# A decoder trunk on one core: another start of the first norm, and the output stored in eight pieces

## The chip, the core and the metric

The kernel runs on one core of one Trainium2 chip. The core has a matrix engine (PE, with its weight loads shown apart as PEld), a vector engine (DVE), a scalar engine (ACT), a general engine (POOL), a sequencer that here only issues transfers (SP), and 16 DMA engines between the chip's memory (HBM) and the core's own memory (SBUF). ACT can issue transfers too, on a queue of its own. PE writes to PSUM, eight banks of 128 x 512 numbers.

The metric is device time in microseconds (us). Of the kernel before there are three timed runs and one profiled execution.

## The reference

Two layers over 256 tokens of width 2048. Each of the four sub-layers (two mixers, two feed-forward blocks) starts with a norm whose scale and shift come from a conditioning row `c`, and ends in a gated residual add. What matters here is the first norm, the row `c`, and the end:

```python
def rms_norm(x, eps=EPS):
    xf = x.astype(jnp.float32)
    return (xf * lax.rsqrt(jnp.mean(xf * xf, -1, keepdims=True) + eps)).astype(x.dtype)

def ada_modulation(c, w, b):
    mod = (jax.nn.silu(c) @ w + b)[:, None, :]
    shift, scale, gate = jnp.split(mod, 3, axis=-1)
    return shift, scale, gate

def reference(x, c, ada_mix_w, ada_mix_b, ...):
    for i in range(DEPTH):
        shift, scale, gate = ada_modulation(c, ada_mix_w[i], ada_mix_b[i])
        h = rms_norm(x) * (1.0 + scale) + shift
        ...                                   # a mixer: h @ w_in, recurrences, @ w_out
        x = x + gate * y
        shift, scale, gate = ada_modulation(c, ada_ffn_w[i], ada_ffn_b[i])
        h = rms_norm(x) * (1.0 + scale) + shift
        x = x + gate * swiglu(h, ffn_w1[i], ffn_w3[i], ffn_w2[i])
    return rms_norm(x) * final_norm_w
```

## The kernel before

The activations lie transposed: 16 tiles (`kt`) of 128 channels x 256 tokens. A product takes a 128 x 128 tile of weights as the stationary operand and 256 tokens as the moving one. For precision each weight tile is split into a high and a low part, `whi` (ACT, a rounding copy) and `wlo` (DVE, a subtraction), and so are the activations (`hhi`, `hlo`); a product is three matmuls: `whi` with `hhi`, `whi` with `hlo`, `wlo` with `hhi`.

**The modulation.** `silc` holds silu(c), the same row of 2048 numbers on all 128 partitions. One modulation value per channel is a multiply-and-sum of a weight row with `silc` on DVE. For the first norm these are 32 tiles of 128 x 2048 (`ini`, 1 MB each, six buffers): for each `kt` one for the scale (a small addition of 1 follows) and one for the shift. The remaining modulations come later, in halves of 1024 columns (`adat`).

**The first stage.** The input `x` arrives in one transfer. ACT squares it tile by tile, PE sums the squares over the channels (the squares are the stationary operand, a block of ones from the constants `cst` the moving one), DVE and POOL raise the sums to the power -1/2 (`rpow`, lines 806 to 809), PE spreads the result over the partitions (`bcast_tok`), ACT copies it to `rb`. From there on, `kt` by `kt`: POOL multiplies `x` by `rb` (`normed`), ACT applies scale and shift and rounds to `hhi`, POOL subtracts to get `hlo` (`first`), and `lin_slab` multiplies with the first 14 weight tiles of that `kt`, which come in two transfers of 7 (448 KB each, four buffers `raw`).

**What sets the order.** Every engine works through its instructions in the order of the program; a wrapper adds that dependence to each call, and so all instructions carry its line, 374, in the profile. The order itself is planned while the program is written out: a list `seq` says in which order the big pieces are loaded and processed (for the first stage: the two `ini` tiles of kt 0, those of kt 1, the two weight pieces of kt 0, the two `ini` tiles of kt 2, the weight pieces of kt 1, and so on). `split_next` processes the next item of that list: for an `ini` tile the multiply-and-sum on DVE, for a weight piece the copy `whi` on ACT; `low_parts` then emits the `wlo` that are due on DVE. `issue_raw` issues the next transfers on SP, strictly in the list's order, when a buffer is free. A cost model (`Clock`, one time per engine) decides between steps that could both come next; its price for a full-precision matmul with 128 stationary columns is

```python
            return max(430.0 if nn < 60 else 214.0, 1.68 * nn)
```

in nanoseconds, where `nn` is the number of moving columns. `split_next(4)` in line 1957 processes the first four `ini` tiles before the squares; the lines from 1961 on are the norm.

**The end.** `rstd_x` makes the last norm's factor in the same manner into a PSUM bank, DVE multiplies `x` by it in four pieces of 128 x 1024, and SP stores each piece.

Of the kernel before, what the change touches and what calls it, by code (L numbers as in the profile page):

```python
# [10 lines left out]
F32 = mybir.dt.float32  # L11
F32R = mybir.dt.float32r
AF = mybir.ActivationFunctionType
ALU = mybir.AluOpType
# [4 lines left out]
P = 128  # L19
T = 256  # L20
KT = 16
# [62 lines left out]
SLAB0, SLAB1, SLABF = len(FIRST0), 7, {0: 14, 1: 8}  # L84
# [50 lines left out]
def halves(n):  # L135

    return [n] if n <= 8 else [(n + 1) // 2, n // 2]
# [260 lines left out]
def trunk(ctx: ExitStack, tc: tile.TileContext, I, out):  # L398
    nc = tc.nc
    clock = Clock()  # L400
    V, S, G, PE, SP = (Ordered(tc, e, clock) for e in (nc.vector, nc.scalar, nc.gpsimd, nc.tensor, nc.sync))
    pool = lambda name, bufs=1, **k: ctx.enter_context(tc.tile_pool(name=name, bufs=bufs, **k))
    cp = pool("cp")
# [10 lines left out]
    def nm(s):  # L414
        uid[0] += 1
        return f"{s}_{uid[0]}"

    def mm(out_, lhsT, rhs, start, stop):
        PE.matmul(out_, lhsT, rhs, start=start, stop=stop)
# [10 lines left out]
    banks = [pp_.tile([P, 512], F32, name=f"bank{q}") for q in range(8)]  # L430
# [5 lines left out]
    def bank(keep=False, spare=SPARE):  # L436

        if keep and len(mine) == 1:
            force(lambda: len(busy) < 8 - spare)
        q = min((q for q in range(8) if q not in busy),  # L440
                key=lambda q: clock.since(bname[q]))
        busy.add(q)
        if not keep:
            mine[-1].append(q)
        return banks[q]
# [48 lines left out]
    def force(stop):  # L494

        while not stop():
            c = min((c for c in chains if not blocked(c)), key=lambda c: c.ready)
            fill_ada(c.ready - IDLE)
            step(c)
# [8 lines left out]
    prm = cp.tile([P, NPRM], F32, name="prm")  # L508
    rows = cp.tile([P, NROW], F32, name="rows")
    silc = cp.tile([P, 2048], F32, name="silc")  # L510
    SP.dma_start(silc, I["crow"].to_broadcast([P, 2048]))
    S.dma_start(x0, I["xT"])
    S.dma_start(cst, I["cst"])
    S.dma_start(prm, I["prm"])
    S.activation(silc, silc, AF.Silu)
    hhi = cp.tile([P, KT, T], F32R, name="hhi")
    hlo = cp.tile([P, KT, T], F32R, name="hlo")
    h2 = (hhi, hlo)
# [1 line left out]
    def K(name, n=None):  # L520
        w = dict(_CST)[name] if n is None else n
        return cst[:, CST[name]:CST[name] + w]
# [4 lines left out]
    ones1 = K("ones", 64)  # L527
    gmask = cst[:, CST["tri"]:CST["tri"] + 384]

    def prc(name, j=0, n=1):  # L530
        return prm[:, COL[name] + j:COL[name] + j + n]
# [4 lines left out]

    half_neg = cp.tile([P, 4], F32, name="half_neg")
    G.memset(half_neg, -0.5)
    half_pos = cp.tile([P, 4], F32, name="half_pos")
    G.memset(half_pos, 0.5)  # L540
    mod = cp.tile([P, 4, 48], F32, name="mod")


# [51 lines left out]
    def issue_raw(upto=-1):  # L595

        while st["raw"] < len(seq):
            it = seq[st["raw"]]
            free, names = (rfree, rname) if it[0] == "w" else (ifree, iname)
            if not free:  # L600
                return
            q = min(free, key=lambda q: clock.since(names[q]))
            if st["raw"] > upto and clock.since(names[q]) > clock.at(ET.PE) + QUEUE:
                return
            free.remove(q)
            if it[0] == "w":
                SP.dma_start(rawt[q][:, :it[2] * P], it[1])
            else:
                l, r, n = it[1:]
                SP.dma_start(init[q], I["ada"][l, 16 * r + n].rearrange("e p f -> p e f"))  # L610
            raws[st["raw"]] = q
            st["raw"] += 1

    def free_raw(q):
        rfree.append(q)
        issue_raw()
# [48 lines left out]
    def split_next(rows=None):  # L665

        while st["item"] < len(seq):
            if rows is not None:
                rows -= 1
                if rows < 0:  # L670
                    return
            i = st["item"]
            issue_raw(i)
            force(lambda: st["raw"] > i)
            it, q = seq[i], raws[i]
            if it[0] == "a":
                raws.pop(i)
                st["item"] += 1
                l, r, n = it[1:]
                t = init[q].rearrange("p e f -> p (e f)")  # L680
                o = mod[:, l, 16 * r + n:16 * r + n + 1]
                V.tensor_tensor_reduce(t, t, silc, 1.0, prc("adab", 48 * l + 16 * r + n), ALU.mult, ALU.add, o)
                if r == 1:
                    V.tensor_scalar(o, o, 1.0, None, ALU.add)
                known.add((l, r, n))
                ifree.append(q)
                issue_raw()
                hook(it[1:4])
                if not after_ada:
                    hook()  # L690
                continue
            n = min(PIECE, it[2] - st["off"])
            if 0 < it[2] - st["off"] - n < PIECE // 2:
                n = (it[2] - st["off"] + 1) // 2
            a, b = st["off"] * P, (st["off"] + n) * P
            hi = wp.tile([P, PIECE * P], F32R, tag="whi", name=nm("whi"), bufs=PARTS)
            lo = wp.tile([P, PIECE * P], F32R, tag="wlo", name=nm("wlo"), bufs=PARTS)
            S.activation(hi[:, :b - a], rawt[q][:, a:b], AF.Copy)
            parts.append((hi, lo, n))
            st["off"] += n  # L700
            end = st["off"] == it[2]
            if end:
                st["off"] = 0
                st["item"] += 1
                raws.pop(i)
            lows.append((hi, lo, a, b, q, end))
            return

    def low_parts():

        while lows:
            hi, lo, a, b, q, end = lows.pop(0)
            V.tensor_tensor(lo[:, :b - a], rawt[q][:, a:b], hi[:, :b - a].bitcast(F32), ALU.subtract)
            if end:
                free_raw(q)
# [3 lines left out]
    def hook(row=None):  # L719

        while hooks and not st["hold"]:
            hooks.pop(0)()
        if row in after_ada:
            hooks.append(after_ada.pop(row))
# [118 lines left out]
    def rstd_x():  # L843
        squares(True)
        ps = bank(True)
        for n in range(2):
            for q in "az":
                mm(ps[:, 64 * n:64 * n + 64], sqa[q][:, n * P:(n + 1) * P], ones1, q == "a", q == "z")
        sqa.clear()
        r = cp.tile([P, 2], F32, tag="rstd", name=nm("rstd"), bufs=2)  # L850
        rpow(r, ps[:, 0:128:64], 2, 1.0 / 2048, EPS)
        release(ps)
        rb = bank(True)
        bcast_tok(rb, r)
        return rb
# [301 lines left out]
    def open_x(name):  # L1157
        xg[name] = tc.tile_pool(name=name, bufs=1, side="right", reuse_waits="tile")
        x = xg[name].__enter__().tile([P, KT, T], F32, name=name)
        xt[name] = x  # L1160
        return x

    def close_x(name):
        xg[name].__exit__(None, None, None)
# [775 lines left out]
    t0 = open_x("tin")  # L1940
# [17 lines left out]
    pq = bank(True)  # L1958
    for kt in range(KT):

        S.activation(t0[:, kt, :], x0[:, kt, :], AF.Square)
    for n in range(2):
        for kt in range(KT):
            mm(pq[:, 64 * n:64 * n + 64], t0[:, kt, n * P:(n + 1) * P], ones1, kt == 0, kt == KT - 1)
    r0 = cp.tile([P, 2], F32, tag="rstd", name=nm("rstd"), bufs=2)
    rpow(r0, pq[:, 0:128:64], 2, 1.0 / 2048, EPS)
    release(pq)
    pq = bank(True)
# [18 lines left out]
    x = layer0(pre_)  # L1987
# [1 line left out]
    layer1(x, "t0b")  # L1989
    ffn(3, x, "t1", None)  # L1990
    rb = rstd_x()
    for q in range(4):
        o = x[:, 4 * q:4 * q + 4, :]
        V.tensor_tensor(o, o, rb[:, 0:T].unsqueeze(1).to_broadcast([P, 4, T]), ALU.mult)
        SP.dma_start(out[:, 4 * q:4 * q + 4, :], o)
    close_x("x0")


# [13 lines left out]
```

## Time and profile before

| | |
|---|---|
| timed runs, median (lowest to highest) | 2975.08 us (2968.41 to 2989.75) |
| profiled execution, its own time | 2977.68 us |
| its span | 2976.0 us |
| PE busy | 2865.2 us, 96% of the span |
| DVE busy | 2176.3 us, 73% |
| ACT busy | 1432.3 us, 48% |
| POOL busy | 218.4 us, 7% |
| DMA | 706.29 MB, mean 237 GB/s |

Busy times are sums over one engine's instructions. PE's instructions overlap, so a busy PE need not be a PE at its best pace. The shares are means over the whole span; the first 140 us, which hold the first norm and the first slab of weights, are read by themselves below. In the views of instructions a row gives start, duration, engine, line, operation, output and inputs, how many instructions were merged, and in brackets the engine's idle time before it with what ended that. In the views of stretches a row gives the busy time of PE, PEld, DVE, ACT and POOL (with the number of instructions), then PE's granted clock, the busy share of the DMA engines and the GB/s they moved.

### The profile page before, as it was taken

The numbers are of one execution on the slowest core, as the hardware profiler recorded it, in microseconds if no ns is written. First come the engines' busy times: TensorE is split into PE (matmuls) and PEld (weight loads), VectorE is DVE, ScalarE is ACT, GpSimd is POOL, SyncE is SP. The second block draws the span as 40 slices with busy tenths as digits, with TensorE's granted clock in tenths as the row PEclk, the third lists the DMA queues.
The fourth block names the chain that finished last, engine by engine and source line by source line (L and its number), as shares of the span: only waits on it lengthen the run. The fifth ranks groups of instructions, "written<-read, shape, count | busy, mean of one in ns | idle before, by whom it ended". The sixth has DMA issues, their size and how long they took to land. (4 is left out here: it accounts for less than half of the span.)

```text
span 2976.0 us, 61340 instructions
## 1 busy us (share of the span) xinstructions
PE 2865.2 (96%) x25114; PEld 2800.0 (94%) x25114; DVE 2176.3 (73%) x3379; ACT 1432.3 (48%) x2363; POOL 218.4 (7%) x250
## 2 busy tenths in 40 slices
PE   6789999998999999999999999999999999999998
PEld 6788898888999999999999999999999999999998
DVE  6987887987878877667688778788867544555454
ACT  3354545544444444444456655554444444444444
POOL 3400001001000000000101001011010000000001
PEclk9999999998999999999999999999999999999999
DMA  9965464587989998788865556676867555555554
GB/s 387 357 203 190 161 207 167 176 279 273 338 278 338 330 310 274 263 272 266 269 228 205 200 200 211 213 250 232 296 224 247 203 180 176 198 189 187 184 177 157
DMA packets 237306, 706.29 MB, mean 237 GB/s; under 512 B 36912, under 2 KB 55648, under 8 KB 236768
## 3 DMA queue, kind: packets, MB, share of 16 engines
q1 hardware_dynamic: 236448, 699.46, 68.3%
q8 instruction: 196, 3.21, 0.4%
q10 hardware_dynamic: 576, 2.92, 0.2%
q14 instruction: 86, 0.70, 0.1%
HBM read 695.70 MB, written 6.58 MB: 236 GB/s over the span
## 5 line engine op out<-in xcount | busy, mean ns | idle before, releaser
L374 DVE TENSOR_TENSOR wlo<-raw,whi 128x1024 fp32r<-128x1024 f32 (+3 forms) x1005 | 1123.8, 1123 | 548.9 <-ACT whi L374 545.8
L374 PE MATMUL bank<-hhi,whi 128*128 128x256 f32 x5568 | 1467.5, 286 | 21.4 <-ACT whi L374 18.1
L374 PE MATMUL bank<-hlo,whi 128*128 128x256 f32 x5568 | 1446.1, 282 | 2.6 <-DVE hlo L374 2.4
L374 ACT ACTIVATE whi<-raw 128x1024 fp32r<-128x1024 f32 (+3 forms) x1005 | 971.6, 972 | 913.0 <-PE bank L374 733.6
L374 PE MATMUL bank<-hhi,wlo 128*128 128x256 f32 x5568 | 1117.4, 283 | 33.3 <-DVE wlo L374 33.0
L374 PEld LDWEIGHTS bank<-hhi,whi 128*128 128x128 f32 x5568 | 1057.3, 190 | 38.4 <-ACT whi L374 21.2
L374 PEld LDWEIGHTS bank<-hlo,whi 128*128 128x128 f32 x5568 | 1057.1, 190 | 6.0 <-DVE hlo L374 3.8
L374 PEld LDWEIGHTS bank<-hhi,wlo 128*128 128x128 f32 x5568 | 855.6, 190 | 42.5 <-DVE wlo L374 39.0
L374 PE MATMUL bank<-ghi,whi 128*128 128x256 f32 x1408 | 351.2, 282 | 0.0
L374 PE MATMUL bank<-glo,whi 128*128 128x256 f32 x1408 | 351.2, 282 | 0.0
L374 PEld LDWEIGHTS bank<-glo,whi 128*128 128x128 f32 x1408 | 265.1, 188 | 0.0
L374 PEld LDWEIGHTS bank<-ghi,whi 128*128 128x128 f32 x1408 | 265.1, 188 | 0.0
L374 PE MATMUL bank<-ghi,wlo 128*128 128x256 f32 x1408 | 229.7, 282 | 0.0
L374 DVE CUSTOM_DVE_ANT_0 adat<-adat,silc,adap 128x1024 f32<-128x1024 f32 x160 | 212.7, 1329 | 21.1 <-DMA adat<-in_ada 20.3
L374 DVE CUSTOM_DVE_ANT_0 adat<-adat,silc,prm 128x1024 f32<-128x1024 f32 x160 | 211.4, 1322 | 14.8 <-DMA adat<-in_ada 14.6
L374 PEld LDWEIGHTS bank<-ghi,wlo 128*128 128x128 f32 x1408 | 193.8, 188 | 0.0
L374 ACT ACTIVATE ghi<-fg 128x256 fp32r<-128x256 f32 x88 | 36.8, 418 | 161.8 <-DVE fg L374 161.8
L374 DVE SCALAR_TENSOR_TENSOR w<-pad,prm,w 128x256 f32<-128x256 f32 x216 | 109.5, 509 | 5.2
L374 DVE CUSTOM_DVE_ANT_0 ini<-ini,silc,prm 128x2048 f32<-128x2048 f32 x32 | 84.7, 2648 | 15.9 <-DMA prm<-in_prm 15.9
L374 DVE SCALAR_TENSOR_TENSOR x<-bank,mod,x 128x256 f32<-128x256 f32 x106 | 50.7, 482 | 49.0 <-PE bank L374 49.0
L374 DVE TENSOR_TENSOR glo<-fg,ghi 128x256 fp32r<-128x256 f32 x88 | 37.4, 425 | 42.6 <-ACT ghi L374 42.6
L374 PE MATMUL bank<-ylo,whi 128*128 128x256 f32 x256 | 67.0, 284 | 0.8 <-DVE ylo L374 0.8
(261 smaller groups left out, 1994.5 us busy)
## 6 DMA issues: line engine op xcount, KB each, us to landing
raw<-in_ffn SPq DMA_DIRECT2D x324, 512.0 KB, 4.2
adat<-in_ada SPq DMA_DIRECT2D x320, 512.0 KB, 5.0
raw<-in_in SPq DMA_DIRECT2D x238, 512.0 KB, 4.1
raw<-in_ffn SPq DMA_DIRECT2D x128, 384.0 KB, 3.8
raw<-in_ffn SPq DMA_DIRECT2D x128, 320.0 KB, 3.3
raw<-in_out SPq DMA_DIRECT2D x75, 512.0 KB, 4.7
ini<-in_ada SPq DMA_DIRECT2D x32, 1024.0 KB, 11.1
raw<-in_in SPq DMA_DIRECT2D x48, 448.0 KB, 4.2
```

Source lines behind the costliest of these rows:

```text
L374: r = f(*a, **k)
```

## The change

- The row `c` is loaded once, to one partition (8 KB), where before it was loaded to all 128 (1 MB). Four matmuls with a stationary row of 0.5 spread it over the partitions, into banks 0 to 3, and four activations of 512 columns with a scale of 2 make `silc` from them. The constant 0.5 is set earlier on POOL for that.
- The parameters `prm` (345.5 KB) are loaded ahead of `x` and of the constants on ACT's queue, where before they were last.
- The sums of squares use 16 columns of ones where before they used 64; the results are read at the same places.
- The two weight pieces of kt 0 are split (`whi` on ACT behind the squares, `wlo` on DVE ahead of `rpow`) where before this was done in `lin_slab`.
- The output is multiplied and stored in eight pieces of 128 x 512, whose transfers are issued by SP and ACT in turn.

```diff
@@ trunk
-    SP.dma_start(silc, I["crow"].to_broadcast([P, 2048]))
+
+    SP.dma_start(silc[0:1, :], I["crow"])
+    S.dma_start(prm, I["prm"])
     S.dma_start(x0, I["xT"])
     S.dma_start(cst, I["cst"])
-    S.dma_start(prm, I["prm"])
-    S.activation(silc, silc, AF.Silu)
+    half_pos = cp.tile([P, 4], F32, name="half_pos")
+    G.memset(half_pos, 0.5)
+    for q in range(4):
+        PE.matmul(banks[q], half_pos[0:1, 0:1].to_broadcast([1, P]), silc[0:1, 512 * q:512 * (q + 1)],
+                  start=True, stop=True)
+    for q in range(4):
+        S.activation(silc[:, 512 * q:512 * (q + 1)], banks[q], AF.Silu, scale=2.0)
...
     half_neg = cp.tile([P, 4], F32, name="half_neg")
     G.memset(half_neg, -0.5)
-    half_pos = cp.tile([P, 4], F32, name="half_pos")
-    G.memset(half_pos, 0.5)
...
         S.activation(t0[:, kt, :], x0[:, kt, :], AF.Square)
+
+    for n in range(len(halves(SLAB0))):
+        split_next()
+    low_parts()
     for n in range(2):
         for kt in range(KT):
-            mm(pq[:, 64 * n:64 * n + 64], t0[:, kt, n * P:(n + 1) * P], ones1, kt == 0, kt == KT - 1)
+            mm(pq[:, 64 * n:64 * n + 16], t0[:, kt, n * P:(n + 1) * P], ones1[:, 0:16], kt == 0, kt == KT - 1)
...
-    for q in range(4):
-        o = x[:, 4 * q:4 * q + 4, :]
-        V.tensor_tensor(o, o, rb[:, 0:T].unsqueeze(1).to_broadcast([P, 4, T]), ALU.mult)
-        SP.dma_start(out[:, 4 * q:4 * q + 4, :], o)
+    for q in range(8):
+        o = x[:, 2 * q:2 * q + 2, :]
+        V.tensor_tensor(o, o, rb[:, 0:T].unsqueeze(1).to_broadcast([P, 2, T]), ALU.mult)
+        (SP, S)[q % 2].dma_start(out[:, 2 * q:2 * q + 2, :], o)
```

## The prediction

> **What bounds the kernel now.** I read the stretches of the first 140 us first, because all parts of the change but one lie there, then the instructions of DVE, ACT and PE in order of time, and the last 10 us at the end.
>
> ```profile
> span 2976.0 us, 61340 instructions
> 10.00:30.00 20.00, 14.81 (x69) 14.62 (x69) 9.81 (x11) 7.02 (x18) 0.70 (x1) 1.00 1.03 413
> 30.00:50.00 20.00, 16.17 (x102) 14.62 (x102) 15.48 (x13) 8.59 (x13) 11.40 (x10) 0.91 0.96 357
> 50.00:130.00 80.00, 60.80 (x457) 58.55 (x455) 79.62 (x78) 31.97 (x44) 40.01 (x20) 0.94 1.03 416
> 132.00:134.00 2.00, 0.64 (x5) 0.64 (x6) 2.00 (x4) 1.02 (x2) 0.48 (x1) 1.00 0.38 154
> ```
>
> From 50 to 130 us DVE is busy 79.62 us of 80 while PE is busy 60.80: DVE sets the pace of the first slab. In the same stretch the DMA engines move 416 GB/s at a busy share of 1.03, so they are full as well. Which of the two would stop first if the other were ahead is the main question. Traffic falls off in the stretch from 132 us: 154 GB/s for 2 us is 0.31 MB, or 0.7 us at 416, so the last `ini` tile has landed at about 132.7.
>
> ```profile
> 15.86 2.35 DVE L374 CUSTOM_DVE_ANT_0 ini<-ini,silc,prm 128x2048 f32<-128x2048 f32 x1 [15.86 <-DMA prm<-in_prm]
> ...
> 23.22 2.35 DVE L374 CUSTOM_DVE_ANT_0 ini<-ini,silc,prm 128x2048 f32<-128x2048 f32 x1
> ...
> 28.04 0.16 DVE L374 TENSOR_SCALAR rpow<-bank 128x2 f32<-128x2 f32 x1 [2.46 <-PE bank L374]
> 34.45 3.03 DVE L374 TENSOR_TENSOR wlo<-raw,whi 128x896 fp32r<-128x896 f32 x2 [6.24 <-ACT whi L374]
> 37.40 2.83 DVE L374 CUSTOM_DVE_ANT_0 ini<-ini,silc,prm 128x2048 f32<-128x2048 f32 x1
> ...
> 42.62 2.09 DVE L374 TENSOR_TENSOR wlo<-raw,whi 128x896 fp32r<-128x896 f32 x2
> 44.62 2.83 DVE L374 CUSTOM_DVE_ANT_0 ini<-ini,silc,prm 128x2048 f32<-128x2048 f32 x1
> ...
> 102.75 2.08 DVE L374 TENSOR_TENSOR wlo<-raw,whi 128x896 fp32r<-128x896 f32 x2
> ...
> 137.17 2.34 DVE L374 CUSTOM_DVE_ANT_0 ini<-ini,silc,prm 128x2048 f32<-128x2048 f32 x1
> ```
>
> These are DVE's instructions, in order of time. It waits 15.86 us for the parameters, works four `ini` tiles until 25.6, waits 2.46 us for the sums of squares (`rpow`), then 6.24 us for the first `whi`, and from 34.45 on hardly waits until the last `ini` tile ends at 137.17 + 2.34 = 139.5. So what the change does to DVE is judged by where the row of 44.62, the first `ini` tile of kt 3, goes: all later work of the slab hangs on it in a closed row, and what comes after the slab is PE's and hangs on the slab.
>
> **The squares and `rpow`.**
>
> ```profile
> 13.53 0.20 ACT L374 ACTIVATE zeros<-cst 128x1 fp32r<-128x1 f32 x1 [0.52 <-DMA cst<-in_cst]
> 13.64 5.00 ACT L374 ACTIVATE tin<-xin 128x256 f32<-128x256 f32 x16
> 30.37 0.38 ACT L374 ACTIVATE rb<-bank 128x256 f32<-128x256 f32 x1 [11.73 <-PE bank L374]
> ...
> 33.48 2.62 ACT L374 ACTIVATE whi<-raw 128x896 fp32r<-128x896 f32 x3
> 14.09 13.92 PE L374 MATMUL bank<-cst,tin 128*128 128x64 f32 x64 [14.09 <-ACT tin L374]
> 158.72 0.61 PE L374 MATMUL bank<-ggg,cst 128*128 128x16 f32 x2 [5.29 <-DVE ggg L374]
> L374 PE MATMUL bank<-ggg,cst x2: 375/385/395, 158.7 to 159.0; 128*128 128x16 f32 x2
> ```
>
> PE needs 13.92 us for 32 sums, two instructions each: 0.2175 us from one instruction to the next. ACT's 16 squares take 5.00 us and are not the limit. Does a block of 16 columns go faster than one of 64? One product of that shape is in the trace, the last two rows: two instructions take 0.61 us together and the second lasts 0.375 to 0.395, so they start 0.215 to 0.235 apart. That is the pace of the 64 columns, and I take it: fewer columns gain nothing, 13.92 us stay. (The bounds: a quarter of it, a gain of 10.4 us on PE, of which ACT's 5.00 us would let through 8.9; and twice as much, the slower rival below.)
>
> When do the squares start? ACT's `zeros`, which waits for `cst`, stands ahead of them in ACT's order, at 13.53. `cst` was second on ACT's queue and becomes last. The queue carries the same three loads, and its last one, `prm`, let DVE go at 15.86; so 15.86 is the late bound for `cst`, 2.3 us later. The 1.05 MB of `silc` no longer compete; had all of them stood ahead, `cst` would come 2.5 us earlier at 413 GB/s, the early bound. I take 14.3, 0.8 later, nearer the late end because the queue's own bytes ahead of `cst` grow. `rpow` then comes at 28.84 instead of 28.04.
>
> **The row `c` and the parameters.**
>
> ```profile
> L374 PE MATMUL bank<-mxw,mbtok 128*128 128x512 f32 x16 | 8.2, 592 | 0.0
> silc<-in_crow SPq DMA_DIRECT2D x1, 1024.0 KB
> 11.26 0.81 SPq L374 DMA_DIRECT2D raw<-in_in  x2
> DMA to landing us min/median/max: 5.1/8.5/11.9
> L374 ACT ACTIVATE mstate<-bank 128x512 f32<-128x512 f32 x8 | 4.8, 595 | 3.3 <-PE bank L374 3.3
> DMA to landing us min/median/max: 3.2/3.3/3.4
> ```
>
> The nearest matmuls to the four new ones are of 512 columns too: 0.51 us an instruction, two a product, so eight take 4.1 us; if PE starts at half that pace, 8.2. ACT takes 0.6 us for 512 columns out of a bank. Small loads (the last row, those of 64 KB through `gscr`) land 3.3 us after issue, and the row is issued first: there at 4 us. So `silc` is ready between 9 and 13 us, and DVE starts then instead of at 15.86, if the first 1 MB of `ini` has landed. That gain of 3 to 7 us is worth nothing by itself: DVE's next fixed point is `rpow`, and it idled 2.46 us ahead of it already. It makes room: the four `ini` tiles are done at the latest at 25.6 as before, more likely at 22, since 1.05 MB fewer at 413 GB/s let all tiles land 2.5 us earlier.
>
> **The first weights split ahead of `rpow`.** The two `whi` go into the 11.73 us in which ACT waits (30.37); two of the three in the row of 33.48 take 1.8 us. The two `wlo` (2.09 us, row of 42.62) go ahead of `rpow` on DVE. `rpow`, and with it POOL, PE and ACT, is now queued behind them. The pieces were issued at 11.26 and 11.65; the latest landing of any piece of the first 60 us took 11.9 us, so they are there at 23.6 at the latest, `whi` ends at 25.4, `wlo` at 26.5, ahead of 28.84. So that wait costs nothing; if the cover were gone, each us of delay would cost one.
>
> What is late next: behind `rpow` DVE now goes straight to the `ini` tiles of kt 2, at 29.0 instead of 37.40. They take 2.35 and 2.83 us with POOL beside them, until 34.3 with their small additions. Then come the `wlo` of kt 1. Their `whi` stand on ACT behind the first two `hhi`, in the place of the row of 33.48, which came 5.44 us after `rpow`: 34.28. The first takes 0.9 us, so `wlo` starts at 35.2, after 0.9 us of waiting, and the pair ends at 37.3. There the first tile of kt 3 starts: 37.3 against 44.62, **7.3 us earlier**. The 6.24 us of waiting go, the two `wlo` of kt 0 move to where DVE idled, and 0.8 us of later `rpow` is paid.
>
> **Can the DMA follow?** The last tile landed at 132.7. It gains 2.5 us from the missing 1.05 MB, and the dip from 30 to 50 us (357 instead of 416 GB/s, 20 us x 59 = 1.18 MB, 2.8 us), which came when DVE stood still and freed no buffer, should close: 127.4. DVE will want it at 137.17 - 7.3 = 129.9. For the weight pieces,
>
> ```profile
> 97.73 2.05 ACT L374 ACTIVATE whi<-raw 128x896 fp32r<-128x896 f32 x2 [1.29 <-DMA raw<-in_in]
> ```
>
> ACT waited for landing and ended at 99.78, with 3.0 us to spare before DVE's `wlo` at 102.75. DVE gets 7.3 ahead, the transfers 5.3, so 2.0 of the 3.0 go. Both margins hold, narrowly. I charge nothing, and take the DMA as the first rival.
>
> **The end.**
>
> ```profile
> 2966.80 1.22 DVE L374 TENSOR_TENSOR x<-x,bank 128x1024 f32<-128x1024 f32 x1 [1.59 <-PE bank L374]
> L374 DVE TENSOR_TENSOR part<-part,bank 128x512 f32<-128x512 f32 x3 | 2.0, 675 | 0.0
> 2968.00:2969.00 1.00, 0.00 (x0) 0.00 (x0) 1.00 (x2) 0.00 (x0) 0.00 (x0) 0.80 0.14 53
> 2973.00:2974.00 1.00, 0.00 (x0) 0.00 (x0) 0.00 (x0) 0.00 (x0) 0.00 (x0) 0.50 1.03 410
> ```
>
> The stores' traffic starts near the end of the first of these two stretches and is still full in the second: the transfer is the limit, not DVE. The first piece is ready after 0.68 us instead of 1.22, so the stores start and end 0.5 us earlier. Bounds: nothing, or a loss of 0.5, if rows of 2 KB move a tenth slower than rows of 4 KB over 5 us; a gain of 1 if the shorter last piece lands sooner. I take 0.5.
>
> **The sum**, against the profiled execution: 2977.68 - 7.3 - 0.5 = 2969.9. That execution lies 2.6 above the median of the runs shown, and so the forecast against that median is 2975.08 - 7.8 = **2967.3**.
>
> **The rivals.**
>
> The DMA is the limit (chance 0.20). With shares of 1.03 from 10 to 30 and from 50 to 130 us it may not catch up the dip; then only the 2.5 us of missing bytes come through, with the dip 5.3. In the middle, with the end: 2975.08 - 3.9 - 0.5 = 2970.7. For it speaks the full share; against it, that the last tile lay landed for 137.17 - 132.7 = 4.5 us.
>
> PE runs the squares at full pace (0.08).
>
> ```profile
> 2964.41 0.39 PE L374 MATMUL bank<-cst,sqacc 128*128 128x64 f32 x2
> 2964.63 0.39 PE L374 MATMUL bank<-cst,sq 128*128 128x64 f32 x2
> ```
>
> At the end of the kernel the same sums take 0.22 us for two instructions, half of the 0.435 at the start. If the four new dense products bring PE to that pace, the squares take 7.0 us and `rpow` waits only for DVE, near 24.5, 4.3 before 28.84; DVE gains up to 7.3 + 4.3 = 11.6, the transfers hold that to about 127.4 + 2.3 = 129.7 for the last tile's end, 9.8 before: 2975.08 - 9.8 - 0.5 = 2964.8. [...]
>
> Narrow products are slow (0.07), the way it gets slower. The kernel's own cost model prices under 60 columns at 430 and 64 at 214: twice. At 0.87 us a sum, the 32 take 27.8 us, `rpow` comes at 42.8, the first `whi` of kt 1 ends at 42.8 + 5.4 + 0.9 = 49.1, `wlo` at 51.3, in place of 44.62: 6.7 later, less 0.5: 2975.08 + 6.2 = 2981.3. It turns from gain to loss where a sum takes 0.435 + 7.3 / 32 = 0.66 us. The row of 158.72 speaks against it.
>
> The planner hands it back (0.15). Its PE clock runs 32 x 216 ns = 6.9 us later after the squares, and banks 0 to 3 are taken earlier; order and banks after the slab may differ. One wait of the length of the row of 158.72 (5.29 us) won or lost: 2975.08 - 7.8 + 5.3 = 2972.6, or 2962.0.
>
> **How the numbers follow.** The forecast (0.50) gives 2967.3. All cases lie between 2962 and 2981.3. The runs shown scatter from 6.7 below to 14.7 above their median, which no case explains; half of each goes to the bounds: low, the planner's better end less some 4 us, 2958; high, the slower rival, 2981.3, which a scatter of 7 above the DMA and planner cases also fills, 2981. A change below 1% (29.8 us), about what a measurement of this kernel can tell from none, holds for every case; outside it only an unforeseen order of the whole program would lead: faster 0.03, same 0.94, slower 0.03.
>
> **What would show it.** Right: DVE's first `ini` tile starts between 9 and 13 us; `whi` and `wlo` of kt 0 lie before `rpow`; `rpow` near 28.8 with 64 matmuls at 0.22 us; the tile of kt 3 near 37.3; the last tile's end near 132; DMA with no dip between 30 and 50. Wrong: DVE waiting for `ini` or for `whi` behind `raw` in the slab (the DMA); a squares row of 7 us or of 28; `rpow` waiting for `wlo`; or the slab earlier and the end not.

## The result and the profile after

The changed kernel takes 2930.10 us (median of 6 runs, 2919.82 to 2947.00). The kernel before, run beside it and counted with the runs shown earlier, takes 2981.69 us (6 runs, 2968.41 to 2989.75). The ratio is 0.9842, with a 95% interval of 0.9816 to 0.9867: 51.6 us less after, where 7.8 were predicted, and the time lies below the predicted range of 2958 to 2981.3 us. The profiled execution after took 2919.82 us, with a span of 2918.0.

The first view is the view of stretches of the kernel after. The columns are those of the prediction: PE, PEld, DVE, ACT and POOL busy with their instructions, granted clock, DMA share, GB/s.

```profile
10.00:30.00 20.00, 13.84 (x64) 13.73 (x64) 13.63 (x14) 7.30 (x20) 1.57 (x1) 1.00 1.02 414
30.00:50.00 20.00, 17.91 (x130) 16.93 (x131) 15.01 (x15) 9.74 (x15) 13.71 (x13) 1.00 1.01 405
50.00:130.00 80.00, 59.88 (x446) 57.70 (x446) 79.62 (x78) 29.50 (x42) 37.62 (x20) 0.91 1.00 404
780.00:880.00 100.00, 100.00 (x885) 100.00 (x884) 81.17 (x110) 50.26 (x70) 0.00 (x0) 1.00 0.87 306
1040.00:1080.00 40.00, 40.00 (x340) 40.00 (x339) 30.59 (x44) 15.99 (x21) 0.00 (x0) 1.00 0.88 301
2300.00:2400.00 100.00, 100.00 (x885) 100.00 (x884) 51.99 (x58) 44.80 (x56) 0.00 (x0) 1.00 0.58 193
```

And the last three of these stretches in the kernel before:

```profile
780.00:880.00 100.00, 100.00 (x855) 100.00 (x854) 77.79 (x106) 48.69 (x68) 0.00 (x0) 1.00 0.86 292
1040.00:1080.00 40.00, 40.00 (x340) 40.00 (x339) 30.16 (x44) 15.88 (x20) 0.00 (x0) 1.00 0.91 300
2300.00:2400.00 100.00, 100.00 (x845) 100.00 (x844) 52.53 (x60) 43.27 (x54) 0.00 (x0) 1.00 0.57 197
```

Between 780 and 880 us, and between 2300 and 2400, PE never stops, before or after, and its granted clock is 1.00. The change touches no instruction there. Yet after it PE starts 885 matmuls in 100 us, one each 113.0 ns, where before it started 855 and 845, one each 117.0 and 118.3 ns. Both stretches belong to products with `hhi` and `hlo`. The stretch from 1040 to 1080 us belongs to products with `ghi` and `glo`, the operands of the feed-forward's second half, and there nothing changed: 340 in 40 us, 117.6 ns.

Is it less waiting? The groups of PE's instructions say no. Before:

```profile
L374 PE MATMUL bank<-hhi,whi 128*128 128x256 f32 x5568 | 1467.5, 286 | 21.4 <-ACT whi L374 18.1
L374 PE MATMUL bank<-ghi,whi 128*128 128x256 f32 x1408 | 351.2, 282 | 0.0
```

After (columns: busy us, mean ns of one | idle time ahead of it, and what ended that):

```profile
L374 PE MATMUL bank<-hhi,whi 128*128 128x256 f32 x5568 | 1437.1, 282 | 22.6 <-ACT whi L374 19.1
L374 PE MATMUL bank<-ghi,whi 128*128 128x256 f32 x1408 | 351.1, 281 | 0.0
```

PE idles as long ahead of the `hhi` products as before, 22.6 us to 21.4. It is the busy time that fell, by 30.4 us in this one of three groups of the kind, and the `ghi` group did not move.

Worked out from the trace, from the first to the last matmul with the named operands (us):

| products with | before | after | less |
|---|---|---|---|
| `hhi`, `hlo` of the first mixer | 34.5 to 986.5 = 952.0 | 35.1 to 971.2 = 936.1 | 15.9 |
| `ghi`, `glo`, first of four parts (the others are alike) | 125.4 | 125.5 | -0.1 |
| `hhi`, `hlo` of the first feed-forward block | 247.9 | 242.0 | 5.9 |
| `hhi`, `hlo` of the second mixer | 623.2 | 608.8 | 14.4 |
| `yhi`, `ylo` | 92.8 | 92.9 | -0.1 |
| `hhi`, `hlo` of the second feed-forward block, two parts | 251.2 + 248.0 | 240.1 + 239.6 | 19.5 |

Some 4 us of the first row are the changed start; nearly all the rest of the gain is spread over the whole kernel wherever `hhi` or `hlo` is an operand.

What sets these two apart from `ghi` and `yhi`? The edit moves a line that reserves memory. `half_pos`, 16 bytes on each partition in a slot of 32, is reserved ahead of `hhi` and `hlo` instead of behind them. So `hhi` begins at byte 31168 of each partition instead of 31136, and `hlo` at 47552 instead of 47520 (addresses of the built programs). `whi`, `wlo`, `ghi`, `glo`, `yhi` and `ylo` lie where they lay, each at a multiple of 128 bytes.

### The profile page after: what moved, and what is told of

The parts are those of the page before. It is cut to its first block, busy times and chain, and to the rows that moved or that the text cites. A ratio compares the mean times of both kernels' runs of the same rounds, so it can differ in the third digit from the quotient of the medians.

```text
span 2918.0 us, 61372 instructions
## 1 busy us (share of the span) xinstructions
PE 2812.5 (96%) x25122; PEld 2741.8 (94%) x25122; DVE 2170.1 (74%) x3383; ACT 1430.5 (49%) x2366; POOL 219.7 (8%) x250
## 5 line engine op out<-in xcount | busy, mean ns | idle before, releaser
L374 PE MATMUL bank<-hhi,whi 128*128 128x256 f32 x5568 | 1437.1, 282 | 22.6 <-ACT whi L374 19.1
L374 PE MATMUL bank<-hlo,whi 128*128 128x256 f32 x5568 | 1415.2, 278 | 4.3 <-DVE hlo L374 3.0
L374 PE MATMUL bank<-hhi,wlo 128*128 128x256 f32 x5568 | 1097.4, 280 | 31.0 <-DVE wlo L374 30.6
L374 PEld LDWEIGHTS bank<-hhi,wlo 128*128 128x128 f32 x5568 | 843.4, 189 | 40.0 <-DVE wlo L374 36.3
```

What stands on the lines that cost most here:

```text
L374: r = f(*a, **k)
```

## The experiments

The theory was that the place of `hhi` and `hlo` sets the pace, and the rival that the changed instructions do, by another order or by work that they trigger later. The first two runs separate these: one has the new place alone, the other all of the new instructions at the old place.

**The new place alone.**

```diff
@@ before
+    half_pos = cp.tile([P, 4], F32, name="half_pos")
     hhi = cp.tile([P, KT, T], F32R, name="hhi")
...
-    half_pos = cp.tile([P, 4], F32, name="half_pos")
     G.memset(half_pos, 0.5)
```

> The kernel before, with one line moved: the tile of the constant 0.5 is reserved ahead of hhi and hlo, so that these two lie 32 bytes further on in SBUF, at 31168 instead of 31136; no instruction, no order and no bank changes. If the place of hhi and hlo makes most of the gain: PE's matmuls with hhi and hlo in the two-projection stretches start 0.113 us apart (443 in 50 us) instead of 0.117 (428), and the time is some 40 to 45 us below before, ratio about 0.986. If the order that the planner made or the choice of banks makes it: no change, ratio 1.000 within 0.002. If it is the new start and end: no change either.

2932.59 us (4 runs), ratio to before 0.9857 (0.9830 to 0.9884): 46.7 us of the gain come from a line that issues nothing. The stretches of this kernel (PE alone: busy, instructions, clock, DMA share, GB/s):

```profile
780.00:880.00 100.00, 100.00 (x882) 1.00 0.88 306
1040.00:1080.00 40.00, 40.00 (x340) 1.00 0.89 303
2300.00:2400.00 100.00, 100.00 (x885) 1.00 0.60 194
```

They are those of the kernel after: 882 and 885, with 340 for `ghi`.

**The new instructions at the old place.**

```diff
@@ after
+    hhi = cp.tile([P, KT, T], F32R, name="hhi")
+    hlo = cp.tile([P, KT, T], F32R, name="hlo")
+    zeros = cp.tile([P, 1], F32R, name="zeros")
+    half_neg = cp.tile([P, 4], F32, name="half_neg")
     half_pos = cp.tile([P, 4], F32, name="half_pos")
...
-    hhi = cp.tile([P, KT, T], F32R, name="hhi")
-    hlo = cp.tile([P, KT, T], F32R, name="hlo")
...
-    zeros = cp.tile([P, 1], F32R, name="zeros")
...
-    half_neg = cp.tile([P, 4], F32, name="half_neg")
```

> The changed kernel with hhi, hlo, zeros and half_neg reserved ahead of the constant 0.5, so that all tiles lie where they lay before; all instructions, their order and their banks are those of the changed kernel. If the place of hhi and hlo makes most of the gain: only the start and the end are left of it, 5 to 9 us, ratio 0.997 to 0.998, and 428 matmuls in 50 us. If planner or banks make it: the whole gain stays, ratio 0.984, 443 in 50 us.

2972.84 us (10 runs), ratio 0.9984 (0.9970 to 0.9999): the whole of what the prediction had costed is worth 6.4 us of 2979.27 by the medians, with an interval from 0.3 to 8.9.

```profile
780.00:880.00 100.00, 100.00 (x836) 1.00 0.84 285
2300.00:2400.00 100.00, 100.00 (x845) 1.00 0.62 203
```

836 and 845: the old pace. The two effects add up, 46.7 + 6.4 = 53.1 us against 51.6 measured for both.

**Which places?** Four more kernels move `hhi` by reserving other small tiles, or the parameter rows, ahead of it or behind it: to 31200, 31232, 30592 and 30656. One diff for all; which lines are moved differs:

```diff
@@ before: 31200 with the first two lines, 31232 with all three
+    half_pos = cp.tile([P, 4], F32, name="half_pos")
+    half_neg = cp.tile([P, 4], F32, name="half_neg")
+    zeros = cp.tile([P, 1], F32R, name="zeros")
     hhi = cp.tile([P, KT, T], F32R, name="hhi")
     hlo = cp.tile([P, KT, T], F32R, name="hlo")
@@ 30592 with the first line, 30656 with all three, and besides
-    rows = cp.tile([P, NROW], F32, name="rows")
...
     hlo = cp.tile([P, KT, T], F32R, name="hlo")
+    rows = cp.tile([P, NROW], F32, name="rows")
```

> The kernel before with the tiles of 0.5 and -0.5 reserved ahead of hhi and hlo: both lie 64 bytes further on, at 31200 and 47584, 32 past a multiple of 64 as before. If a start on a multiple of 64 bytes is what counts: the old pace, 0.117 us a matmul, and the time of before within 0.4%. If only the old place was bad: 0.113 us and some 40 us less.

> The kernel before with the tiles of 0.5, -0.5 and zeros reserved ahead of hhi and hlo: both lie 96 bytes further on, at 31232 and 47616, multiples of 64, 128 and 256. If a start on a multiple of 64 is what counts: 0.113 us a matmul and some 40 us less than before. If it is the place within 128 or 256 bytes (the fast one lies 64 past a multiple of 128, while ghi, at a multiple of 128, goes at 0.118): the old pace, 0.117, and no gain.

> The kernel before with the tile rows reserved behind hhi and hlo and that of 0.5 ahead: hhi and hlo start at 30592 and 46976, multiples of 128, 896 past a multiple of 1024. If the place within 128 bytes decides: slow, 0.117 to 0.120 us a product with hhi or hlo. If any place away from that of the weights over 1024 bytes is fast: 0.113. If a start on a multiple of 64 were enough, it would be fast too, but 31232 has spoken against that.

> The kernel before with rows reserved behind hhi and hlo, and the tiles of 0.5, -0.5 and zeros ahead: hhi and hlo start at 30656 and 47040, 64 past a multiple of 128 and 192 past one of 256, but 960 past one of 1024. If the place within 128 or 256 bytes decides: fast, 0.113 us, some 45 us below before. If the place over 1024 bytes, against the weights, decides: slow, 0.117 to 0.120.

One run each: 2989.28 us at 31200, 3001.84 at 31232, 2990.19 at 30592, 2945.02 at 30656. The row of 780 to 880 us of each, in this order:

```profile
780.00:880.00 100.00, 100.00 (x848) 1.00 0.86 294
```

```profile
780.00:880.00 100.00, 100.00 (x836) 1.00 0.85 283
```

```profile
780.00:880.00 100.00, 100.00 (x845) 1.00 0.87 290
```

```profile
780.00:880.00 100.00, 100.00 (x885) 1.00 0.88 303
2300.00:2400.00 100.00, 100.00 (x851) 1.00 0.56 187
```

Only 30656 has 885, and it is, like 31168, 64 bytes past a multiple of 128. The others are 96, 0 and 0 past one, and 31136 is 32 past. But 30656 did not hold the pace: 851 in the later stretch.

**The same for `ghi`.** If this is right, `ghi` and `glo` are at a bad place in both kernels.

```diff
@@ after; a second kernel reserves [P, 208], 832 bytes
+            fp.tile([P, 16], F32, name=f"gpad{l}")
             ghi = fp.tile([P, NHH, T], F32R, name=f"ghi{l}")
```

> The changed kernel with 64 unused bytes ahead of ghi and glo, so that they start at 120512 and 143040, 64 past a multiple of 128 (192 past one of 256), like hhi and hlo in the changed kernel; nothing else differs. If the place within 128 or 256 bytes decides: the products with ghi and glo go at 0.113 us instead of 0.1187, 4224 of them, 23 us less than the changed kernel, ratio to before about 0.976. If the place against that of the weights (whi, wlo), seen over 1024 bytes, decides, or something that belongs to hhi and hlo alone: no change from the changed kernel, ratio 0.984.

> The changed kernel with 832 unused bytes ahead of ghi and glo: they start at 121280 and 143808, at 448 past a multiple of 1024, where hhi and hlo of the changed kernel stand too, and 64 short of where whi and wlo stand. If the place within 1024 bytes, that is against the weights, decides: products with ghi and glo at 0.113 us instead of 0.1187. If the place within 128 bytes decides: 121280 is 64 past a multiple of 128, so 0.113 as well, and only the run with 64 bytes tells the two apart. If neither: 0.1187.

With 64 bytes 2912.45 us (4 runs), ratio to before 0.9757 (0.9724 to 0.9791), below both kernels; with 832 bytes 2912.29 (one run). The stretch of `ghi`, first with 64 and then with 832 bytes:

```profile
1040.00:1080.00 40.00, 40.00 (x356) 1.00 0.94 324
```

```profile
1040.00:1080.00 40.00, 40.00 (x355) 1.00 0.93 327
```

356 and 355 instead of 340: 112.4 and 112.7 ns a product.

**The place itself, or the distance from the weights?** In all kernels so far `whi` and `wlo` lay at multiples of 128. So "64 past a multiple of 128" and "64 from the weights, modulo 128" could not be told apart. The next kernel moves the weights.

```diff
@@ after
     adat = [wp.tile([P, 1024], F32, name=f"adat{q}") for q in range(ADAS)]
+    wp.tile([P, 16], F32, name="wpad")
```

> The changed kernel with 64 bytes reserved behind the adat tiles. hhi and hlo stay where the changed kernel has them (64 bytes past a multiple of 128); the weight pieces whi and wlo, until now at multiples of 128, and everything behind them (ini, ghi, glo, yhi, ylo) move 64 bytes up. Theory A, what counts is the place of the streamed operand (hhi, ghi) by itself: hhi products stay at 113.3 ns (885 in 100 us) and ghi products go to 113.3 as well (355 in 40 us instead of 339), about 2912 us. Theory B, what counts is the distance of the streamed operand from the weights: hhi products fall back to 118 to 120 ns (836 to 855 in 100 us) and ghi products stay at 118.7, about 2972 us.

2988.42 us (one run), 16 us more than theory B expected; the pace decides between the two.

```profile
780.00:880.00 100.00, 100.00 (x845) 1.00 0.86 289
1040.00:1080.00 40.00, 40.00 (x340) 1.00 0.89 304
2300.00:2400.00 100.00, 100.00 (x845) 1.00 0.63 205
```

`hhi` has not moved, and its products are back at 845; `ghi` has moved to 64 past a multiple of 128, and gains nothing, since the weights have moved with it. The theory of the place itself falls. Its mirror image settles it: the operands at multiples of 128, the weights 64 past one.

```diff
@@ after; zeros and half_neg are reserved ahead of hhi, which comes to 31232
+    wp.tile([P, 16], F32, name="wpad")
...
+            fp.tile([P, 16], F32, name=f"gpad{l}")
             ghi = fp.tile([P, NHH, T], F32R, name=f"ghi{l}")
...
+                fp.tile([P, 16], F32, name="ypad1")
                 yhi = fp.tile([P, KT, T], F32R, name="yhi1")
```

> The changed kernel with all places mirrored: hhi and hlo at multiples of 128 bytes, the weight pieces whi and wlo 64 bytes past one, ghi, glo, yhi and ylo at multiples of 128 again. By the theory that the place of the streamed operand itself counts (64 past a multiple of 128 is fast), every product is slow: about 836 to 855 in 100 us and some 2985 us. By the theory that only the distance between streamed operand and weights counts (64 bytes, modulo 128, is fast), every product is as fast as with ghi and yhi moved up: 113.3 to 117.7 ns, about 2906 us.

2912.18 us (4 runs), ratio 0.9802 (0.9757 to 0.9846).

```profile
780.00:880.00 100.00, 100.00 (x885) 1.00 0.88 302
1040.00:1080.00 40.00, 40.00 (x356) 1.00 0.93 316
2300.00:2400.00 100.00, 100.00 (x885) 1.00 0.59 193
```

At 31232, where `hhi` gave 836 with the weights at multiples of 128, it gives 885 with the weights 64 bytes on. It is the distance.

**All operands at 64 from the weights.** The weights stay, and `yhi` gets its 64 bytes too.

```diff
@@ after
+            fp.tile([P, 16], F32, name=f"gpad{l}")
             ghi = fp.tile([P, NHH, T], F32R, name=f"ghi{l}")
...
+                fp.tile([P, 16], F32, name="ypad1")
                 yhi = fp.tile([P, KT, T], F32R, name="yhi1")
```

> The changed kernel with 64 bytes reserved ahead of ghi and another 64 ahead of yhi, so that every streamed operand, ghi, glo, yhi and ylo too, begins 64 bytes past a multiple of 128. By the theory that the place sets the pace, the 768 products with yhi and ylo gain 768 x 5.4 ns = 4 us on the kernel with ghi moved alone (2912 us): about 2908, and the stretch in which they run shows 113.3 ns. By the theory that only the total layout matters, no further gain.

2905.83 us (5 runs, 2899.71 to 2921.30), ratio to before 0.9744 (0.9721 to 0.9767): the shortest of all. The products with `yhi` took 2093.1 to 2182.0 = 88.9 us in its trace, where they took 92.9 after: the 4 us expected. In the whole time the step from 2912.45 is within the two intervals. The profiled execution was the longest of the five, and shows that the distance does not settle everything:

```profile
780.00:880.00 100.00, 100.00 (x851) 1.00 0.86 284
1040.00:1080.00 40.00, 40.00 (x342) 1.00 0.90 307
2300.00:2400.00 100.00, 100.00 (x885) 1.00 0.61 195
```

From 731 to 1477 us this trace has 6335 starts of `hhi`, `hlo`, `ghi` and `glo` products in one unbroken chain, 117.8 ns apart on average and all but one slow; from 2080 us on 7202 of 7208 are at 114 ns or less, with the same tiles. Before 700 us, 2000 of 2995 were at 114 ns or less too. The trace's starts, counted over each whole execution (start to next start within one kind of product; those over 123 ns, some 500 of `hhi` and `hlo`, are left out):

| kernel | distance of `hhi`, of `ghi` (bytes, modulo 128) | `hhi`, `hlo`: up to 114 ns, 115 to 123 ns | `ghi`, `glo`: up to 114, 115 to 123 |
|---|---|---|---|
| before | 32, 0 | 48, 15954 | 29, 4191 |
| after | 64, 0 | 13565, 2432 | 0, 4220 |
| new place alone | 64, 0 | 12903, 3038 | 0, 4220 |
| new instructions, old place | 32, 0 | 3, 15966 | 3, 4217 |
| `hhi` at 31200 | 96, 0 | 4, 15949 | 53, 4167 |
| `hhi` at 31232 | 0, 0 | 88, 15827 | 91, 4129 |
| `hhi` at 30592 | 0, 0 | 130, 15827 | 0, 4220 |
| `hhi` at 30656 | 64, 0 | 10379, 5557 | 0, 4220 |
| `ghi` moved by 64 | 64, 64 | 11959, 3991 | 3165, 1055 |
| `ghi` moved by 832 | 64, 64 | 11171, 4844 | 3165, 1055 |
| weights moved | 0, 0 | 133, 15803 | 0, 4220 |
| mirror | 64, 64 | 11565, 4400 | 4212, 8 |
| all at 64 | 64, 64 | 9557, 6430 | 2110, 2110 |
| after, 64 columns again (below) | 64, 0 | 11207, 4789 | 0, 4220 |
| after, without the early split (below) | 64, 0 | 10894, 5072 | 0, 4220 |

At the distances 0, 32 and 96 under 1 in 40 reach 114 ns. At 64 half to all of them do. That a whole quarter (1055 of 4220) or half of `ghi` stays out points to a second condition, met or missed for a whole block of products at a time.

The traces show when it is decided. In the nine with `hhi` at 64, take the unbroken rows of at least 60 products at that distance: one operand pair (`hhi` and `hlo`, say), no start more than 123 ns after the one before. There are 340. Read in groups of ten starts, 235 rows are fast and 105 slow, and none changes its pace after its first ten. So whether a row is fast or slow is settled where it starts, behind a wait, other matmuls or a change of operand, and holds until the next break. What settles it was not found.

**Two parts of the start.** One kernel takes 64 columns again in the 32 sums; the other leaves out the early split.

```diff
@@ after, one kernel
-            mm(pq[:, 64 * n:64 * n + 16], t0[:, kt, n * P:(n + 1) * P], ones1[:, 0:16], kt == 0, kt == KT - 1)
+            mm(pq[:, 64 * n:64 * n + 64], t0[:, kt, n * P:(n + 1) * P], ones1, kt == 0, kt == KT - 1)
@@ after, the other
-    for n in range(len(halves(SLAB0))):
-        split_next()
-    low_parts()
```

> The changed kernel with 64 columns again in the 32 sums of the first norm. If narrow products cost as much as those of 64 columns, as the prediction had it, the squares' row stays at 13.8 to 13.9 us, rpow stays within 0.2 us of 28.1 and the tile of kt 3 near 40.4. If the 16 columns do save time, the squares' row and rpow come later, up to 24 us and 38.

> The changed kernel without the call that splits the first weights ahead of the sums; hhi stays at its new place, so the pace of its products is as in the changed kernel. By the prediction's working the splits then stand behind rpow again and DVE's first tile of kt 3 comes 5 to 7 us later than with them, at 45 to 47 us instead of 40.4, with the kernel some 5 us longer (2925 to 2935). If the early split's gain is taken by POOL's slow rstd (2.67 us beside DVE's tile, 0.70 without), then rstd falls back to 0.70 us here and the tile comes only 2 to 4 us later.

One run each, 2933.66 and 2941.88 us (2925 to 2935 was expected of the second), both within the scatter of the kernel after, so the rows decide. With 64 columns:

```profile
14.70 13.91 PE L374 MATMUL bank<-cst,tin 128*128 128x64 f32 x64 [4.78 <-ACT tin L374]
```

The squares last 13.91 us, with 16 columns 13.84 (below): the columns are worth 0.07 us. `rpow` comes at 28.65 and the tile of kt 3 at 40.93, 0.5 us later than after; `rpow` so misses the expected 28.1 by more than 0.2, but the squares themselves began 0.46 us later (14.70 instead of 14.24). Without the early split, on DVE:

```profile
28.20 0.16 DVE L374 TENSOR_SCALAR rpow<-bank 128x2 f32<-128x2 f32 x1 [5.50 <-PE bank L374]
34.60 3.02 DVE L374 TENSOR_TENSOR wlo<-raw,whi 128x896 fp32r<-128x896 f32 x2 [6.24 <-DMA ini<-in_ada]
44.76 2.82 DVE L374 CUSTOM_DVE_ANT_0 ini<-ini,silc,prm 128x2048 f32<-128x2048 f32 x1
```

and on POOL:

```profile
28.51 0.70 POOL L374 TENSOR_TENSOR rstd<-rpow,half_neg 128x2 f32<-128x2 f32 x1 [27.64 <-DVE rpow L374]
```

The tile of kt 3 comes at 44.76, as before the change (44.62): without the early split nothing is left of what the start gains. `rstd` is back at 0.70 us, from the 2.67 of the kernel after. The 4.35 us between 40.41 (after) and 44.76 lie between the two expectations: POOL's slower step, 1.97 us longer with the early split, takes part of the gain, not most of it.

## Why the prediction was wrong

**The step that failed is the sum itself**, 2977.68 - 7.3 - 0.5. It has a term for each instruction that is added, removed or moved, and none for the pace of the 16,704 products that stay. It took a moved reservation for nothing: `half_pos` is seen only as a constant that is set earlier. So the statement that a change below 1% "holds for every case" was wrong: the time fell by 1.6%, and by that limit faster had only 0.03. No rival held a change of pace. In place of the missing term the runs measured 46.7 us (the new place alone). The profile before held a hint: 855 and 845 starts in 100 us show that the pace of one and the same kind of product is not fixed. A list of what each tile's address becomes would have asked the question; the size could not have been read from this trace.

**The first stage: right in its mechanism, too large in its size.** DVE after, in order of time:

```profile
12.20 2.35 DVE L374 CUSTOM_DVE_ANT_0 ini<-ini,silc,prm 128x2048 f32<-128x2048 f32 x1 [12.20 <-DMA ini<-in_ada]
...
28.12 0.16 DVE L374 TENSOR_SCALAR rpow<-bank 128x2 f32<-128x2 f32 x1 [3.61 <-PE bank L374]
28.19 2.34 DVE L374 CUSTOM_DVE_ANT_0 ini<-ini,silc,prm 128x2048 f32<-128x2048 f32 x1
30.65 2.34 DVE L374 CUSTOM_DVE_ANT_0 ini<-ini,silc,prm 128x2048 f32<-128x2048 f32 x1
36.49 1.48 DVE L374 TENSOR_TENSOR wlo<-raw,whi 128x896 fp32r<-128x896 f32 x1 [3.49 <-ACT whi L374]
39.40 1.09 DVE L374 TENSOR_TENSOR wlo<-raw,whi 128x896 fp32r<-128x896 f32 x1 [1.44 <-ACT whi L374]
40.41 2.85 DVE L374 CUSTOM_DVE_ANT_0 ini<-ini,silc,prm 128x2048 f32<-128x2048 f32 x1
...
132.92 2.34 DVE L374 CUSTOM_DVE_ANT_0 ini<-ini,silc,prm 128x2048 f32<-128x2048 f32 x1
```

`rpow` comes at 28.12 (28.84 predicted), the `ini` tiles of kt 2 right behind it, and the tile of kt 3 at 40.41: 4.2 us earlier than before, not 7.3. The last tile starts at 132.92 instead of 137.17, so the 4.2 us reach the end of the slab. The 3.1 us that lack are in two rows that were not foreseen, one of POOL and one of ACT:

```profile
28.43 2.67 POOL L374 TENSOR_TENSOR rstd<-rpow,half_neg 128x2 f32<-128x2 f32 x1 [27.56 <-DVE rpow L374]
```

```profile
35.52 0.93 ACT L374 ACTIVATE whi<-raw 128x896 fp32r<-128x896 f32 x1
38.42 0.95 ACT L374 ACTIVATE whi<-raw 128x896 fp32r<-128x896 f32 x1 [1.96 <-PE bank L374]
```

First, POOL's small `rstd` took 0.70 us as long as DVE idled behind `rpow`. Its row before:

```profile
28.35 0.70 POOL L374 TENSOR_TENSOR rstd<-rpow,half_neg 128x2 f32<-128x2 f32 x1 [27.49 <-DVE rpow L374]
```

Now DVE goes straight on to an `ini` tile, and beside that `rstd` takes 2.67. Everything behind it, `rb`, `hhi` and the first `whi` of kt 1 (35.52, predicted 34.28), is late by that. The other traces agree: 0.70 without the early split, where DVE idles 6.24 us behind `rpow`, and 2.67 with 64 columns, with the weights moved and with all at 64, where DVE goes straight on. What makes `rstd` slow there was not shown. Second, the next `whi` waits 1.96 us for PE to let go of a buffer, and `wlo` waits behind it. The prediction priced the pair of `wlo` at 2.1 us in one piece; it took 40.41 - 36.49 = 3.92. The size of that wait is not fixed: in the trace of the new instructions at the old place PE starts its first products 0.213 us apart until 40.7 us, the second `whi` waits 3.53 us for it, and the tile of kt 3 comes at 42.19, only 2.4 us earlier than before. What slowed PE there was not looked into.

**The squares and the row `c`: right in cost, and the rivals fall.** PE after:

```profile
2.50 7.16 PE L374 MATMUL bank<-silc,half_pos 1*128 1x512 f32 x8 [2.50 <-DMA silc<-in_crow]
14.24 13.84 PE L374 MATMUL bank<-cst,tin 128*128 128x16 f32 x64 [4.58 <-ACT tin L374]
```

The 64 instructions keep 0.216 us each, so narrow products are neither quicker nor twice as slow, and the four products of 7.16 us did not bring PE to the pace of the same kind of sums at the kernel's end (0.22 us for two instructions, 2906.64 to 2906.86) for the squares, which start 4.58 us behind them. The first `ini` tile starts at 12.20 (DVE's row above), inside 9 to 13; it waits for its own transfer.

**The DMA follows.** From 30 to 50 us 405 GB/s instead of 357, the dip is gone; from 50 to 130 DVE is busy 79.62 of 80 us, as before, and from 45 to 135 us it never waits for a transfer. So the DMA did not set the 4.2 us; whether it would have followed 7.3 was not tested. **The planner**: no loss is seen, but none is ruled out. The new instructions at the old place are 6.4 us ahead over the whole kernel; the interval of 0.3 to 8.9 holds the predicted 7.8, and the planner rival's 7.8 - 5.3 = 2.5 too.

**The end** gains less than 0.5 us:

```profile
2909.03 4.87 DVE L374 TENSOR_TENSOR x<-x,bank 128x512 f32<-128x512 f32 x8 [1.59 <-PE bank L374]
```

From this start to the end of the span are 2918.0 - 2909.03 = 8.97 us, before 2976.0 - 2966.80 = 9.20: 0.2 us.

## What to carry to other kernels

A moved reservation is a change like any other: compare the addresses of the large tiles before and after an edit, and before explaining a difference by the instructions, run a kernel with the new order at the old addresses and one with the old order at the new ones. Where PE never stops, count its starts in a stretch far from the edit, before and after; a different count there is no matter of the edit's own steps. Where matmuls are back to back, a pad of 64 bytes ahead of the streamed operand is cheap to try: here the change alone gave the ratio 0.9842, with one such pad on top 0.9757, with two 0.9744. Count over the whole trace, though: in the nine traces each of the 105 rows of products that started slow stayed slow until its next break, so one stretch can mislead.

## What the runs showed of the hardware

The pace of a stream of fp32r matmuls of 128 x 256, each with its own weight load, depended on where the streamed operand lies relative to the weights: 113 ns from start to start for half to all of a trace's products where the two are 64 bytes apart modulo 128, and 117 to 120 ns where they are 0, 32 or 96 apart, at a granted clock of 1.00 in every stretch compared. Moving the weights by 64 bytes, with `hhi` left where it was, took its products from 885 to 845 starts in 100 us, so the pace of the stream does not hang on its own place alone. What lies behind that was not seen, only that the distance counts. Nor was it found what decides, where an unbroken row of products starts, whether it runs at 113 or at 118 ns at the good distance; 340 rows kept to the one or the other. That may be behind the scatter of the kernel after, 2919.82 to 2947.00 us; only one execution of each kernel was traced, so that is not shown.
